# A mixer's projection products interleaved across units, and the k multiply of a level ahead of its copies

## The chip, the cores and the metric

The kernel runs on one core of a Trainium2 chip. The metric is the device time of one launch in microseconds, the median of several runs. TensorE (PE in the profile) does matmuls into eight PSUM banks of 128x512 f32, VectorE (DVE) and ScalarE (ACT) empty them, GpSimd (POOL) does further elementwise work, and SyncE (SP) issues most of the DMAs. Each engine runs its own list of instructions in order and waits on semaphores for the others.

## The reference

One layer on 2048 rows of width 1024: a norm and one input projection, two mixers on its columns, gates, an output projection, and a gated feed-forward network. Cut to what matters here:

```python
D_MODEL, SEQ, DEPTH = 1024, 2048, 1
def layer(x):
    z = rmsnorm(x, g) @ W_in            # [pool u | q | f | v | output gate | branch gates]
    a = pool_mixer(u, pool_w, pool_scale)      # trailing means over 2, 4, 8, 16 rows, less the row
    h = hgrn2_mixer(q, f, v, o, lb, norm_g)    # 4 heads: S_t = diag(f_t) S_{t-1} + (1-f_t) v_t^T
    m = sigmoid(ga) * (a @ W_pa) + sigmoid(gb) * (h @ W_pb)
    x = x + m @ W_out
    x = x + (silu(conv(n @ W_gate)) * conv(n @ W_val)) @ W_down    # n = rmsnorm(x, g2)
    return x
```

Inside the second mixer the decay between two rows is the product of the f between them, so attention within a chunk needs q and k scaled by running products of f.

## The kernel before, in words

The 2048 rows are worked in two passes of 1024, `b0` = 0 and 2, each of two halves of 512 rows. A pass runs a mixer and then the feed-forward part. Products of large matrices are made in units of the seven-product kind: a 2x2 block product from seven products P1 to P7 of sums of blocks, instead of eight. Each product is twelve matmuls of 128x512, since every operand is split in a high and a low fp32r part.

**The projections** of a mixer are 14 such units in the order of `PROJ` (L55): `fq` (f and q of a head), `g` (gates) and `u` (pool input). Before the change a unit runs through `ORDER` (L52): P1 P6 P5 P7 P2 P4 P3. P1 and P2 use one PSUM bank (X), P6, P7 and P4 a second (Z), P5 and P3 a third (V), and a bank gathers. `Unit.multiply` (L1172) issues a product and `Unit.after` (L1191) what follows it: behind P1, ACT copies e1 out of X (L1194); behind P6, VectorE makes u2 = e1 - Z (L1196); behind P7, u3 = Z - e1 (L1200) and one result, u3 + V (L1159). P7 adds into the bank that u2 reads, so it waits for u2; P4 waits for u3 in the same way.

**Weights** come as a stream (class `Stream`, L168): a load of 128x512 into one of 8 places (`raw`), in the first pass for some products a sum of blocks on POOL (L444), and then a split: ACT's cast to the high part (L231) and VectorE's subtract for the low part (L232), into a ring of 6 places (`ops`). A place comes free when the product that used it has ended. `plan_mixer` lists in which order the stream delivers. The second pass reads back the sums that the first one stored.

**Tasks** run between the products. After every sixth matmul of `mm` (L148) a tick steps the stream and each task. `hgrn_task` (L965) has a task for a head and a half: levels 1, 2, 4-8, 16-32 and 64 combine ever larger blocks of rows. At each level TensorE multiplies k and the scaled q into a bank (`pl`), VectorE copies pieces of it under masks into the attention matrix (`at`), and multiplies q, k and the decays (f) for the next level. `two_levels` (L993) does levels 4 and 16, in two pairs of banks, `pl.._0` and `pl.._2`. Behind the levels come `pk` (k transposed), `pv`, the states `ss`, the outputs `po`, their scaling `ot` (L1138) and a transpose `pt` (L1144). The pool's tasks make window sums `s` (L934), `p` (L939), its split `pl_g` (L657), and the product `pm`, and store `mx`.

**The end of the projections.** From the last unit on, `pa_task` loads the pool results again (`mx`, L961) and splits them (`mxs`, L656, L657), and the branch products `pa` and `pb`, chains of twelve matmuls, follow.

Names of tiles end in the half and the head or the group: `ur0_0` is unit u of group 0 in the first pass, `pl1_0_16_2` level 16 of head 0 in half 1, its second pair. In the profile the numbers are left out.

**The order on each engine** is made by a scheduler: it walks the program, simulates a timeline and puts each engine's instructions in the order in which they would become ready. Dependencies ahead of a task's product (`in_turn`, `first`, `behind`) pin some of it.

## Time and profile before

| what | us |
|---|---|
| median of 3 runs (2533.47 to 2534.64) | 2533.51 |
| the profiled execution, its own time | 2532.39 |
| its span in the profile | 2530.7 |
| projections of the first mixer, 98.15 to 454.70 | 356.55 |
| projections of the second mixer, 1358.90 to 1705.50 | 346.60 |

The granted clock of TensorE is 0.999 over the span. In the rows of the profile a line gives the engine, the line of the kernel, the operation, what is written and read (without numbers), shape and count; in a timeline the start and the time of the group stand first, and the square bracket holds the idle time before it and the engine that ended it. Matmuls overlap by their pipelining, so the steps from start to start count, not a record's own duration. The two windows hold the projections and what runs beside them; the second ends with the first `pa` chains.

### The profile page before, as it was taken

Reading aid. Unit: us, or ns where it says so; the run is one execution under the profiler, and the core shown is the slowest. Engines: PE = TensorE matmul, PEld = TensorE weight load, DVE = VectorE, ACT = ScalarE, POOL = GpSimd, SP = SyncE. Lnnn points to the kernel's source line nnn. Section 1 sums busy time; section 2 is a strip of 40 time slices with the busy share of each in tenths; the row PEclk is TensorE's granted clock in tenths of the full one; section 3 lists DMA queues with packets and bytes.
Section 4 is the critical chain, followed back from the end, with each engine's and each line's share of the span. In section 5 each row is a group of like instructions: output and inputs, shape, how many; then the busy total and the mean of one; then the engine's idle time right before and its main releaser. Section 6 shows DMA issues by size and latency. Waiting matters only on the chain.

```text
span 2530.7 us, 35649 instructions
## 1 busy us (share of the span) xinstructions
PE 2509.1 (99%) x11508; PEld 2053.6 (81%) x11508; DVE 1978.5 (78%) x3508; ACT 1176.1 (46%) x2218; POOL 753.4 (30%) x1127
## 2 busy tenths in 40 slices
PE   9999999999999999999999999999999999999998
PEld 7888888788888888888888888888888888888886
DVE  7889878598898777885596778765979888778755
ACT  6534343334555454554554343442355554445534
POOL 4344453003354334451320202200033432325410
PEclk9999999999999999999999999999999999999999
DMA  8878777777898879897344343446443454447852
GB/s 270 272 180 233 202 206 231 219 230 244 199 260 228 229 230 241 261 366 243 124 147 150 112 132 108 139 146 225 149 155 117 151 154 135 152 134 245 321 166 97
DMA packets 252332, 493.76 MB, mean 195 GB/s; under 512 B 26544, under 2 KB 43056, under 8 KB 251824
## 3 DMA queue, kind: packets, MB, share of 16 engines
q1 hardware_dynamic: 184512, 313.60, 39.1%
q0 software_dynamic: 42656, 112.74, 17.6%
q10 hardware_dynamic: 24976, 65.13, 7.6%
q8 instruction: 91, 1.49, 0.2%
q14 instruction: 97, 0.79, 0.1%
HBM read 381.79 MB, written 187.17 MB: 225 GB/s over the span
## 4 chain that ended last, share of the span: by engine, by line
PE 91%; DVE 5%; issue 1%; DMA 1%; POOL 1%; ACT 1%; SPq 0%; DVEq 0%; POOLq 0%; ACTq 0%
PE dn_P L148 16%; PE up_Z L148 14%; PE up_X L148 10%; PE up_V L148 10%; PE wo_P L148 6%; PE gr_Z L148 4%; PE pb L148 4%; PE pa L148 3%; PE io_Z L148 3%; PE gr_X L148 3%; PE fr_Z L148 2%; PE gr_V L148 2%; PE io_V L148 2%; PE fr_X L148 2%; PE fr_V L148 2%; PE pl L1026 1%
## 5 line engine op out<-in xcount | busy, mean ns | idle before, releaser
L231 ACT CAST ops<-raw 128x512 fp32r<-128x512 f32 x744 | 459.7, 620 | 817.8 <-PE dn_P L148 177.4
L232 DVE TENSOR_TENSOR ops<-raw,ops 128x512 fp32r<-128x512 f32 x744 | 553.0, 747 | 216.3 <-ACT ops L231 208.4
L1614 DVE SCALAR_TENSOR_TENSOR e<-h,cols,e 128x512 f32<-128x512 f32 x176 | 143.2, 818 | 30.9 <-ACT e L1612 26.3
L1612 ACT ACTIVATE e<-h,cols 128x512 f32<-128x512 f32 x176 | 142.3, 814 | 25.1 <-DVE h L1159 18.2
L1617 DVE SCALAR_TENSOR_TENSOR e<-h,cols,e 128x512 f32<-128x512 f32 x176 | 133.9, 770 | 2.5
L961 POOL DMA_DIRECT2D g_P<-dg_P x154 | 83.8, 545 | 160.3 <-PE dn_P L148 114.1
L1269 POOL TENSOR_TENSOR gf_P<-e,e 128x512 f32<-128x512 f32 x44 | 61.2, 1392 | 150.4 <-DVE e L1623 96.2
L1269 POOL TENSOR_TENSOR gf_P<-gf_P,e 128x512 f32<-128x512 f32 x44 | 59.1, 1344 | 72.0 <-DVE e L1623 71.5
L1409 POOL TENSOR_TENSOR q<-q,qs 128x512 f32<-128x512 f32 x16 | 21.7, 1357 | 185.2 <-ACT qs L1408 178.7
L1607 POOL COPY h<-h 128x2 f32<-128x2 f32 x88 | 40.8, 476 | 117.3 <-DVE h L1158 110.4
L1446 ACT ACTIVATE gt<-gt,cols 128x512 f32<-128x512 f32 x48 | 34.8, 725 | 86.8 <-DVE gt L1159 71.5
L1621 ACT ACTIVATE e<-e 128x512 f32<-128x512 f32 x88 | 55.6, 632 | 38.9 <-DVE e L1617 38.7
L1609 POOL COPY hist<-h 128x2 f32<-128x2 f32 x88 | 35.0, 398 | 117.6 <-DVE h L1159 115.8
L1159 DVE TENSOR_TENSOR h<-up_u,up_V 128x512 f32<-128x512 f32 x88 | 60.0, 682 | 10.2 <-PE up_V L148 9.7
L1244 DVE TENSOR_TENSOR x<-x,wo_P 128x512 f32<-128x512 f32 x88 | 56.0, 680 | 12.1 <-PE wo_P L148 11.9
L1244 DVE TENSOR_TENSOR ac<-ac,dn_P 128x512 f32<-128x512 f32 x72 | 47.1, 681 | 16.7 <-PE dn_P L148 16.5
L1011 POOL COPY qm<-q 128x64 f32<-128x64 f32 x64 | 29.9, 494 | 96.2 <-issue 25.9
L1026 PE MATMUL pl<-qm,k 128*128 128x192 f32 x256 | 50.6, 327 | 3.7 <-DVE k L1047 3.5
L1637 POOL DMA_DIRECT2D dg_P<-gf_P x88 | 50.7, 576 | 8.3 <-POOL gf_P L1269 7.4
L1607 POOL COPY h<-hist 128x2 f32<-128x2 f32 x88 | 45.0, 518 | 27.4 <-DVE m_T42l L657 27.3
L1194 ACT COPY up_e<-up_X 128x512 f32<-128x512 f32 x44 | 25.8, 586 | 58.2 <-PE up_X L148 53.1
L1026 PEld LDWEIGHTS pl<-qm,k 128*128 128x128 f32 x256 | 43.9, 189 | 9.6 <-POOL u L925 2.2
(1285 smaller groups left out, 8088.0 us busy)
## 6 DMA issues: line engine op xcount, KB each, us to landing
g_P<-dg_P POOLq DMA_DIRECT2D x154, 256.0 KB, 6.2
raw<-in_w_up_t SPq DMA_DIRECT2D x132, 256.0 KB, 3.2
raw<-in_w_in_t SPq DMA_DIRECT2D x98, 256.0 KB, 3.5
dg_P<-gf_P POOLq DMA_DIRECT2D x88, 256.0 KB, 4.0
dg_P<-e SPq DMA_DIRECT2D x66, 256.0 KB, 3.6
raw<-in_w_dn SPq DMA_DIRECT2D x66, 256.0 KB, 3.9
x<-in_x SPq DMA_DIRECT2D x64, 256.0 KB, 4.9
gd<-gt ACTq DMA_DIRECT2D x64, 256.0 KB, 3.2
```

The lines of the kernel that those rows point to most:

```text
L148: count[1] = pe.matmul(*args, **kw)
L231: self.mark = act.copy(hi, v)
L232: low = self.low = dve.tensor_tensor(lo, v, f32(hi), ALU.subtract)
L961: eng.dma_start(t, d)
L1026: ins = pe.matmul(pa_[:, c * 192 : c * 192 + 192], ks[:, (i + c) * P : (i + c + 1) * P], mv[:, c].rearrange("p s x -> p (s x)"), start=Tru ...
L1159: return dve.tensor_tensor(dst, t, ps, ALU.add if how == "add" else ALU.subtract)
L1244: dve.tensor_tensor(t, t, ps[j], ALU.add if sg > 0 else ALU.subtract)
L1269: pin(eng.tensor_tensor(t, x0, x1, op))
L1607: pool.tensor_copy(h[:, 0:2], hist[:, mt] if hf == 0 else hs[s, 0][:, TB : TB + 2])
L1612: in_turn(act.activation(t, h[:, 2:], AF.Identity, bias=col(o_cb + mt), scale=col(o_cw + 4 * MF + mt)))
L1614: in_turn(second(dve.scalar_tensor_tensor(t, h[:, 1 : 1 + TB], col(o_cw + 2 * MF + mt), t, ALU.mult, ALU.add)))
L1617: dve.scalar_tensor_tensor(t, h[:, 0:TB], col(o_cw + mt), t, ALU.mult, ALU.add)
```

## The change

Three edits in one file. The list `UNITS` gives the order of all the products of a mixer: P1 of the first unit, and then for each unit P6 P5 P2 P7, P1 of the next unit, P4 P3. The last unit keeps P6 P5 P7 P2 P4 P3. Two products stand between P6 and P7 in place of one, and between P7 and P4 the next unit's P1. The weight plan walks the same list. `pa_task` starts behind P6 of the last unit and no longer behind its P1, since P1 now lies in the unit before.

In `two_levels` the q multiply and the small products of decays move ahead of the `pl` products, to the operands; the k multiply is cut in two halves, each right behind its pair of `pl`, and the masked copies come after both. At levels 1, 2 and 64 the k multiply comes first, q and the decays follow, then the copies, with the two copies in the other order.

```diff
+UNITS = [(0, "P1")]
+for _n in range(len(PROJ) - 1):
+    UNITS += [(_n, "P6"), (_n, "P5"), (_n, "P2"), (_n, "P7"), (_n + 1, "P1"), (_n, "P4"), (_n, "P3")]
+UNITS += [(len(PROJ) - 1, p) for p in ORDER[1:]]
...
-        for kind, i in PROJ:
-            if (kind, i) == ("u", 0):
-                plan_one("pw", pool_wt)
-            plan_unit("in", w_in_t, kind, i, ORDER, b0)
+        units = {}
+        for n, p in UNITS:
+            kind, i = PROJ[n]
+            if n not in units:
+                if (kind, i) == ("u", 0):
+                    plan_one("pw", pool_wt)
+                mv, mg = proj_tiles(kind, i)
...
+            fn, raws = units[n][p]()
+            stream.op("in", fn, raws)
...
+            dve.tensor_tensor(qq[:, :, 1, :], qq[:, :, 1, :],
+                              dd[:, :, 0, 0:1].to_broadcast(full), ALU.mult)
+            dve.tensor_tensor(dd[:, :, 2, 0:1], dd[:, :, 2, 0:1], dd[:, :, 3, 0:1], ALU.mult)
+            dve.tensor_tensor(dd[:, :, 1, 0:1], dd[:, :, 1, 0:1], dd[:, :, 2, 0:1], ALU.mult)
+            dve.tensor_tensor(dd[:, :, 0, 0:1], dd[:, :, 0, 0:1], dd[:, :, 1, 0:1], ALU.mult)
             yield AHEAD
...
                 yield 1
+                half = slice(i * nb, (i + 2) * nb)
+                dve.tensor_tensor(kk[:, half, 0:3, :], kk[:, half, 0:3, :],
+                                  dd[:, half, 1:4, 0:1].to_broadcast([P, 2 * nb, 3, hh]),
+                                  ALU.mult)
+            for i, ps in zip(range(0, NT, 2), pls):
+                cc = slice(i, i + 2)
                 dve.copy_predicated(av[:, cc, :, 1, :], mask(hh, 2),
                                     ps[:, :, 0].rearrange("p c (b h) -> p c b h", h=hh))
...
-            if lv < 2:
-                dve.copy_predicated(av[:, :, :, 1, :], mask(hh, NT), pv4)
...
+            dve.tensor_tensor(k3[:, :, 0, :], k3[:, :, 0, :],
+                              d3[:, :, 1, 0:1].to_broadcast(full), ALU.mult)
             if lv:
                 dve.tensor_tensor(q3[:, :, 1, :], q3[:, :, 1, :],
                                   d3[:, :, 0, 0:1].to_broadcast(full), ALU.mult)
-            dve.tensor_tensor(k3[:, :, 0, :], k3[:, :, 0, :],
-                              d3[:, :, 1, 0:1].to_broadcast(full), ALU.mult)
             dve.tensor_tensor(d3[:, :, 0, 0:1], d3[:, :, 0, 0:1], d3[:, :, 1, 0:1], ALU.mult)
+            if lv < 2:
+                pv4 = pa_.rearrange("p (c s x) -> p c s x", c=NT, s=2)
+                dve.copy_predicated(av[:, :, :, 1, :], mask(hh, NT),
+                                    pv4[:, :, 0].rearrange("p c (b h) -> p c b h", h=hh))
+                dve.copy_predicated(ad, masks[-1 - lv].to_broadcast([P, NT, 64]), pv4[:, :, 1])
...
-        for n, (kind, i) in enumerate(PROJ):
...
-            for p in ORDER:
-                u.multiply(p, forms, late)
-                u.after(p)
-                if n == len(PROJ) - 1 and p == "P1":
-                    quiet[0] = True
-                    mtask = Task(pa_task())
+        units = {}
+        for n, p in UNITS:
...
+            units[n].multiply(p, forms, late)
+            units[n].after(p)
+            if (n, p) == (len(PROJ) - 1, "P6"):
+                quiet[0] = True
+                mtask = Task(pa_task())
```

Lines of the changed kernel stand some five to ten further down: u2 L1205, u3 L1209, the split L236 and L237, k L1049, the copies L1054 and L1057, `ot` L1147, `pt` L1153, the window sum L939 and p L944.

Three places of the engines' orders. First VectorE at level 16 of head 0 in the first mixer; `at0_0` and `at1_0` are the attention matrices of the two halves, `k0_0` and `k1_0` their k. Before:

```order
247 L1037 COPY_PREDICATED at0_0_1456<-m129_1144,pl0_0_16_0_1808 128x4x32
248 L1034 COPY_PREDICATED at1_0_1470<-m16_976,pl1_0_16_0_1811 128x8x16
249 L232 TENSOR_TENSOR ops50_1839<-raw49_1428,ops50_1839 128x512
250 L1037 COPY_PREDICATED at0_0_1456<-m128_1119,pl0_0_16_0_1808 128x4x32
251 L1037 COPY_PREDICATED at1_0_1470<-m129_1144,pl1_0_16_0_1811 128x4x32
252 L1034 COPY_PREDICATED at0_0_1456<-m16_976,pl0_0_16_2_1823 128x8x16
253 L1047 TENSOR_TENSOR k0_0_1453<-k0_0_1453,f0_0_1390 128x8x48
254 L1034 COPY_PREDICATED at1_0_1470<-m16_976,pl1_0_16_2_1829 128x8x16
255 L1037 COPY_PREDICATED at1_0_1470<-m128_1119,pl1_0_16_0_1811 128x4x32
256 L1047 TENSOR_TENSOR k1_0_1467<-k1_0_1467,f1_0_1436 128x8x48
```

After:

```order
249 L1049 TENSOR_TENSOR k0_0_1471<-k0_0_1471,f0_0_1361 128x4x48
250 L1054 COPY_PREDICATED at0_0_1474<-m16_976,pl0_0_16_0_1833 128x8x16
251 L1057 COPY_PREDICATED at0_0_1474<-m129_1144,pl0_0_16_0_1833 128x4x32
252 L1049 TENSOR_TENSOR k1_0_1485<-k1_0_1485,f1_0_1455 128x4x48
253 L1054 COPY_PREDICATED at1_0_1488<-m16_976,pl1_0_16_0_1836 128x8x16
254 L1057 COPY_PREDICATED at0_0_1474<-m128_1119,pl0_0_16_0_1833 128x4x32
255 L1057 COPY_PREDICATED at1_0_1488<-m129_1144,pl1_0_16_0_1836 128x4x32
256 L1057 COPY_PREDICATED at1_0_1488<-m128_1119,pl1_0_16_0_1836 128x4x32
257 L1049 TENSOR_TENSOR k0_0_1471<-k0_0_1471,f0_0_1361 128x4x48
258 L1054 COPY_PREDICATED at0_0_1474<-m16_976,pl0_0_16_2_1847 128x8x16
```

The whole k (128x8x48) of a half stood behind the copies of the first pair and behind one copy of the second; a half of k (128x4x48) now stands first behind each pair, and each pair's three copies behind it.

Second VectorE at unit f1 of the first mixer; `p1_0`, its low part `pl1_0l` and the next sum `s1_1_2` are the pool's, `fr0_1_u3` is what P4 of the unit waits for. Before:

```order
286 L939 SCALAR_TENSOR_TENSOR p1_0_2076<-s1_0_1_1975,u1_0_1959 128x512
287 L1117 SCALAR_TENSOR_TENSOR st0_1_123<-ss0_0_2061,f0_0_1390,pv0_0_2056 128x128
288 L232 TENSOR_TENSOR ops56_2041<-w56s4_2038,ops56_2041 128x512
289 L232 TENSOR_TENSOR ops57_2073<-raw53_1704,ops57_2073 128x512
290 L657 TENSOR_TENSOR pl1_0l_2079<-p1_0_2076,pl1_0h_2078 128x512
291 L934 TENSOR_TENSOR s1_1_2_2082<-s1_1_1_1979 128x512
292 L1200 TENSOR_TENSOR fr0_1_u3_2091<-fr0_1_Z_2003,fr0_1_e1_2001 128x512
293 L1159 TENSOR_TENSOR q1_1_2093<-fr0_1_u3_2091,fr0_1_V_2031 128x512
```

After:

```order
294 L237 TENSOR_TENSOR ops58_2109<-w58s2_2106,ops58_2109 128x512
295 L237 TENSOR_TENSOR ops59_2142<-w58s1_2103,ops59_2142 128x512
296 L237 TENSOR_TENSOR ops60_2189<-raw56_1831,ops60_2189 128x512
297 L944 SCALAR_TENSOR_TENSOR p1_0_2112<-s1_0_1_2005,u1_0_1990 128x512
298 L662 TENSOR_TENSOR pl1_0l_2115<-p1_0_2112,pl1_0h_2114 128x512
299 L939 TENSOR_TENSOR s1_1_2_2118<-s1_1_1_2009 128x512
300 L1209 TENSOR_TENSOR fr0_1_u3_2126<-fr0_1_Z_1992,fr0_1_e1_1928 128x512
301 L1168 TENSOR_TENSOR q1_1_2128<-fr0_1_u3_2126,fr0_1_V_2033 128x512
```

`p1_0` stood ahead of a state (`st0_1`) and two splits; now it stands behind three splits, and its low part, the next sum and u3 follow it directly.

Third VectorE at the end of the first mixer's projections; `ot0_3` and `ot1_3` are the outputs of head 3 in the two halves, `ops` the low parts of splits, `mxs` those of the pool results. Before:

```order
787 L232 TENSOR_TENSOR ops132_4937<-raw98_4603,ops132_4937 128x512
788 L657 TENSOR_TENSOR mxs1_1l_4845<-mx1_1_4842,mxs1_1h_4844 128x512
789 L1138 SCALAR_TENSOR_TENSOR ot0_3_4854<-po0_3_4769,ro0_3_4784,z0_3_4703 128x128 x4
790 L1159 TENSOR_TENSOR gt1_0_7_4877<-gr0_7_u2_4674,gr0_7_V_4676 128x512
791 L657 TENSOR_TENSOR mxs1_2l_4885<-mx1_2_4882,mxs1_2h_4884 128x512
792 L657 TENSOR_TENSOR mxs1_3l_4891<-mx1_3_4888,mxs1_3h_4890 128x512
793 L1519 TENSOR_TENSOR ya0_0_4924<-gl0_0_0_4894,pa0_0_4906 128x512
794 L232 TENSOR_TENSOR ops133_5014<-raw99_4660,ops133_5014 128x512
795 L232 TENSOR_TENSOR ops134_5053<-raw100_4689,ops134_5053 128x512
796 L1138 SCALAR_TENSOR_TENSOR ot1_3_4957<-po1_3_4859,ro1_3_4874,z1_3_4787 128x128 x4
```

After:

```order
807 L662 TENSOR_TENSOR mxs1_2l_4878<-mx1_2_4875,mxs1_2h_4877 128x512
808 L662 TENSOR_TENSOR mxs1_3l_4884<-mx1_3_4881,mxs1_3h_4883 128x512
809 L237 TENSOR_TENSOR ops133_5021<-raw99_4662,ops133_5021 128x512
810 L1147 SCALAR_TENSOR_TENSOR ot0_3_4917<-po0_3_4806,ro0_3_4821,z0_3_4737 128x128 x4
811 L1530 TENSOR_TENSOR ya0_0_4940<-gl0_0_0_4887,pa0_0_4899 128x512
812 L1530 TENSOR_TENSOR ya0_4_4964<-gl0_0_4_4891,pa0_4_4946 128x512
813 L237 TENSOR_TENSOR ops134_5069<-raw100_4699,ops134_5069 128x512
814 L1147 SCALAR_TENSOR_TENSOR ot1_3_4988<-po1_3_4922,ro1_3_4937,z1_3_4824 128x128 x4
```

`ot0_3` stood behind `ops132`, and both `ops133` and `ops134` between it and `ot1_3`; now it stands behind `ops133`, and `ops134` alone is ahead of `ot1_3`.

More of the change, by code (lines that the diff above doesn't have):

```diff
@@ L390, in plan_io @@
                 stream.op("io", fn, raws)
-    def plan_unit(key, src, kind, i, order, b0):
-        mv, mg = proj_tiles(kind, i)
-        if b0:
-            unit = sums_of_unit(src, mv, mg, lambda p: lambda: kept["in", (kind, i), SUM_OF[p]])
-        else:
-            unit = weights_of_unit(src[mv], src[mg], (kind, i))
-        for p in order:
-            fn, raws = unit[p]()
-            stream.op(key, fn, raws)
     def plan_mixer(b0):
         plan_io(b0)
-        for kind, i in PROJ:
-            if (kind, i) == ("u", 0):
-                plan_one("pw", pool_wt)
-            plan_unit("in", w_in_t, kind, i, ORDER, b0)
+        units = {}
[5 more added lines that the diff above has]
+                mv, mg = proj_tiles(kind, i)
+                if b0:
+                    units[n] = sums_of_unit(w_in_t, mv, mg, lambda p, u=(kind, i): (
+                        lambda: kept["in", u, SUM_OF[p]]))
+                else:
+                    units[n] = weights_of_unit(w_in_t[mv], w_in_t[mg], (kind, i))
+            fn, raws = units[n][p]()
+            stream.op("in", fn, raws)
         for key, src in (("pa", w_pa_t), ("pb", w_pb_t)):
@@ L1473, in mixer @@
         mixed, oT = {}, {}
[L1474 to L1483 removed]
+        units = {}
+        for n, p in UNITS:
+            kind, i = PROJ[n]
+            if n not in units:
+                if (kind, i) == ("u", 0):
+                    held["w"] = stream.get("pw")
+                units[n] = Unit(f"{kind[0]}r{b0}_{i}", "in", emits[kind](i))
+            units[n].multiply(p, forms, late)
[3 more added lines that the diff above has]
+                mtask = Task(pa_task())
         def branch(key, s, xs, evac, each):
```

25 lines of the change are left out of this document (6 added, 19 removed).

## The prediction

> **What bounds the kernel now.** I read the page first: busy times and the chain of waits.
>
> ```profile
> PE 2509.1 (99%) x11508; PEld 2053.6 (81%) x11508; DVE 1978.5 (78%) x3508; ACT 1176.1 (46%) x2218; POOL 753.4 (30%) x1127
> ...
> PE 91%; DVE 5%; issue 1%; DMA 1%; POOL 1%; ACT 1%; SPq 0%; DVEq 0%; POOLq 0%; ACTq 0%
> ```
>
> TensorE is busy 2509.1 of 2530.7 us and carries 91% of the chain, VectorE 5%. The change adds and removes no product, so it can win only time in which TensorE stands still: 21.6 us in the whole execution. Next came a table of stages, for the two stretches that the change reorders, the projections of the first mixer and of the second.
>
> ```profile
> core 0: us, PE busy (x) PEld busy (x) DVE busy (x) ACT busy (x) POOL busy (x), PEclk, DMA share, GB/s
> 98.15:454.70 356.55, 351.11 (x1777) 292.08 (x1776) 299.33 (x679) 142.59 (x320) 143.13 (x151) 1.00 0.78 218
> 1358.90:1705.50 346.60, 346.52 (x1770) 291.13 (x1769) 258.01 (x665) 143.64 (x317) 59.17 (x86) 1.00 0.43 129
> ```
>
> The columns are the stretch, its length and the busy time of each engine. The first mixer leaves TensorE 5.4 us idle (356.55 less 351.11), the second 0.1. The prize therefore lies in the first mixer, where VectorE is busy 84% of the time and POOL makes the weight sums that the second mixer only reads back. The waits of TensorE in that stretch (total, times, longest) name its releasers.
>
> ```profile
> PE pl L1026 <- DVE k L1047: 3.5, 2, 1.8
> PE ur_Z L148 <- DVE ur_u L1196: 1.1, 1, 1.1
> PE gr_Z L148 <- DVE gr_u L1200: 0.4, 1, 0.4
> PE fr_Z L148 <- DVE fr_u L1196: 0.3, 1, 0.3
> ```
>
> The second mixer has no such row. Two kinds of wait carry the loss: the level products `pl` for the k multiply, and P7 for u2.
>
> **The k multiply.** One of the two places in order of time:
>
> ```profile
> 150.08 1.31 POOL L444 TENSOR_TENSOR w51s<-raw,raw 128x512 f32<-128x512 f32 x1 [1.53 <-issue]
> 150.13 1.29 DVE L1046 TENSOR_TENSOR f<-f 128x8 f32<-128x8 f32 x1
> 151.76 1.26 DVE L1045 TENSOR_TENSOR f<-f 128x8 f32<-128x8 f32 x1
> ...
> 152.94 0.28 DVE L1037 COPY_PREDICATED at<-m,pl 128x128 f32<-128x128 uint8 x1
> 153.13 0.28 DVE L1034 COPY_PREDICATED at<-m,pl 128x128 f32<-128x128 uint8 x1
> 153.33 0.55 DVE L1047 TENSOR_TENSOR k<-k,f 128x384 f32<-128x384 f32 x1
> ...
> 154.02 0.89 PE L1026 MATMUL pl<-qm,k 128*128 128x192 f32 x4 [1.77 <-DVE k L1047]
> 154.40 0.16 DVE L1049 TENSOR_TENSOR f<-f 128x8 f32<-128x8 f32 x1
> ```
>
> VectorE runs without a gap here: two multiplies of 8 columns take 1.29 and 1.26 us beside POOL's sum, where a like one alone takes 0.16. Two masked copies (0.28 each) then stand ahead of k, which ends at 153.88, and TensorE has waited 1.77. The other place shows the same figure (3.5 for two). The change puts k ahead of the copies, gives it the first half of the operands only, and takes the q multiply and the small decays off the piece between. I price the removal at 3.8: at least the 3.5 of the view, at most 4.3, since the view counts from a modelled matmul end.
>
> The split adds instructions. A half has 192 columns; the nearest rows are the whole k (384 columns, mean 682 ns) and the q multiply of 128 columns (295).
>
> ```profile
> L1047 DVE TENSOR_TENSOR k<-k,f 128x384 f32<-128x384 f32 x16 | 10.9, 682 | 0.0
> ...
> L939 DVE SCALAR_TENSOR_TENSOR p<-s,u 128x512 f32<-128x512 f32 x8 | 6.2, 773 | 2.5 <-DMA kwfq1ins<-w53s 2.1 <-PE pm L949 0.4
> ...
> L1043 DVE TENSOR_TENSOR q<-q,f 128x128 f32<-128x128 f32 x16 | 4.7, 295 | 0.0
> ...
> L657 DVE TENSOR_TENSOR pl_1l<-p,pl_1h 128x512 fp32r<-128x512 f32 x2 | 1.4, 692 | 0.1
> ```
>
> Between them a half is about 0.39, two halves 0.1 more than the whole: 16 multiplies add 1.6 us of VectorE to a stage in which it has 57 us free. That is hidden, except where VectorE has no slack. Such places remain: the copies, now last, are what gives the level's PSUM bank back. In head 0 the changed order puts 39 VectorE instructions between the first `pl` of level 4 and the bank's release for the last of level 16. At the undisturbed durations of the rows (0.16 for a small decay, 0.28 a copy, 0.39 a half of k, 0.68 a split or u2) they come to about 12.4 us, an estimate, against 12.7 us of matmul steps on TensorE, so one hit of 1.1 us by a POOL sum (1.29 less 0.16 above) shows. Heads 0 and 3 run their two sequences side by side in this way. I charge 0.8 for each, 1.5 in all; bounds 0 (no hit) to 3.5 (the old wait by another name).
>
> **u2 and P7.** The largest of these waits:
>
> ```profile
> 308.67 0.39 PE L148 MATMUL ur_V<-x_T13h,ops 128*128 128x512 f32 x1
> 308.90 0.39 PE L148 MATMUL ur_V<-x_T13l,ops 128*128 128x512 f32 x1
> ...
> 310.02 0.62 DVE L1037 COPY_PREDICATED at<-m,pl 128x128 f32<-128x128 uint8 x2
> 310.55 0.68 DVE L1196 TENSOR_TENSOR ur_u<-ur_e,ur_Z 128x512 f32<-128x512 f32 x1
> ...
> 311.29 0.50 PE L148 MATMUL ur_Z<-x_T30h,ops 128*128 128x512 f32 x1 [1.11 <-DVE ur_u L1196]
> ```
>
> Products step by 0.23 us a matmul (308.67 to 308.90), so twelve take 2.8. u2 starts at 310.55, behind copies, and P7 at 311.29 instead of about 310.2. With P5 and P2 both between P6 and P7, u2 has 2.8 us more. The largest lateness is 1.1, so the wait goes everywhere: 1.4 by the view (1.1 and 0.3), and up to 2.4, as 1.0 more of TensorE's 5.4 idle us has no other name; I take 1.8. P4's distance to u3 stays one product, since P1 of the next unit takes the place that P2 had: the 0.4 of `gr_u` L1200 stays.
>
> **What comes in its place.** The new order also moves the tasks that run between the products. Four places lose cover.
>
> First, the last unit's transposes. Before, one column group of `pt` waits behind two weight splits whose ring place comes free only at the end of a `pa` chain:
>
> ```profile
> 464.23 1.14 ACT L231 CAST ops<-raw 128x512 fp32r<-128x512 f32 x2 [3.25 <-PE pa L148]
> 464.88 1.29 DVE L232 TENSOR_TENSOR ops<-raw,ops 128x512 fp32r<-128x512 f32 x2 [2.58 <-ACT ops L231]
> ...
> 466.09 1.12 DVE L1138 SCALAR_TENSOR_TENSOR ot<-po,ro,z 128x128 f32<-128x128 f32 x4
> 466.49 0.33 PE L1144 MATMUL pt<-ident,ot 128*128 128x128 f32 x1 [1.84 <-DVE ot L1138]
> ```
>
> From the cast (464.23) to `pt` (466.49) are 2.26 us, of which TensorE idles 1.84. After the change this place has a long cover, but `ot0_3` stands behind one such split and `pt0_3` directly behind the `pa1_0` that frees it: one cast, one subtract, one `ot`, thus 2.26 less the second subtract's 0.6, or 1.65, and the distance is nil. I take 1.7, bounds 1.2 to 1.9. In the first mixer this replaces 1.84 (net -0.1); in the second mixer `ot2_3` and `pt2_3` stand in the same way and nothing is given back: +1.7.
>
> Second, P4 of unit g4. Its u3 stands behind a window sum. Before:
>
> ```profile
> 342.85 0.70 DVE L934 TENSOR_TENSOR s<-s 128x524 f32<-128x524 f32 x1
> ...
> 343.59 0.69 DVE L1200 TENSOR_TENSOR gr_u<-gr_Z,gr_e 128x512 f32<-128x512 f32 x1
> ...
> 343.99 0.39 PE L1127 MATMUL po<-st,q 128*128 128x128 f32 x2
> ...
> 344.21 0.39 PE L1125 MATMUL po<-v,at 128*128 128x128 f32 x2
> ...
> 344.35 0.48 PE L148 MATMUL gr_Z<-x_T40h,ops 128*128 128x512 f32 x1
> ```
>
> From the sum's start to P4 are 1.50 us, and TensorE was just not late. In the changed order this sum waits for the last of `po0_2`, with two steps of 0.22 us (343.99 to 344.21) and the product's own between: 0.67 of cover. I charge 1.0; bounds 0 (if the sum's input has been free longer) to 1.5.
>
> Third, P4 of unit f1: p, its cast, its low part, the next sum and u3 now follow `po0_0` in one queue: 0.77, about 0.62 (a cast, 464.23 above, two in 1.14), 0.69, 0.70 and 0.69 from the rows, with some 0.2 of hand-over 3.7 us, against 2.5 us of `pv`, `po` and `pm` steps. +1.2; bounds 0 to 1.5.
>
> Fourth, the `mx` loads start one product later, because their task now starts at P6 of the last unit.
>
> ```profile
> 454.29 0.68 DVE L232 TENSOR_TENSOR ops<-raw,ops 128x512 fp32r<-128x512 f32 x1
> ...
> 455.42 0.88 SPq L961 DMA_DIRECT2D mx<-md  x2
> ...
> 459.69 0.62 ACT L656 CAST mxs_2h<-mx 128x512 fp32r<-128x512 f32 x1 [0.94 <-DMA mx<-md]
> ...
> 460.34 0.69 DVE L657 TENSOR_TENSOR mxs_2l<-mx,mxs_2h 128x512 fp32r<-128x512 f32 x1 [2.36 <-ACT mxs_2h L656]
> ```
>
> ```profile
> DMA to landing us min/median/max: 2.9/4.2/5.1
> ```
>
> Before, the third load is issued behind a split's subtract (454.29) at 455.42 and its low part is ready at 461.03, 5.6 us on. That split is paced by the last product of the unit in both orders: a cast of 0.62 and three VectorE steps of 0.6 lie between, so I estimate 2.5 from the unit's end to the issue, and 8.1 to the part. `pa1_0` comes after two whole `pa` chains and eight `po` steps (2.8 + 2.8 + 1.8) and needs the part in its seventh or eighth matmul, at 9.0, when it has been ready for 0.9 us; the next part follows 0.7 us after it, with half a microsecond to spare. With the longest landing (5.1 against 4.3 from 455.42 to 459.69) that one is late by 0.3. I charge 0.3 for both mixers; bounds 0 to 4.
>
> The SP queue is otherwise moved only with the products that pace it, and so are POOL's sums, which follow the stream in the new order of use.
>
> **The sum.** -3.8 -1.8 -0.1 +1.7 +1.0 +1.2 +1.5 +0.3 = 0.0. The profiled execution took 2532.39 us (span 2530.7), 1.1 under the median of the runs, 2533.51; the difference is put on that median: **2533.5 us**. With each term at its bound nearest to gain the sum is -6.1 (-4.3 -2.4 -0.6 +1.2), nearest to loss +7.6 (-3.5 -1.4 +0.1 +1.9 +1.5 +1.5 +3.5 +4).
>
> **The rivals.**
>
> The new waits don't come. What speaks for it: each of the four rests on durations in one queue, and a term falls where that queue has run ahead. Against: the two splits at the `pa` end are freed by the very chain that `pt` follows. With the two `ot` waits alone: -3.8 -1.8 -0.1 +1.7, or 2529.5; with the second mixer's away too, 2527.8.
>
> VectorE becomes the bound in the level stretches of the first mixer: slower. Place: heads 0 and 3, levels 4 to 16 and 16 to 64, four stretches. A POOL sum that meets both halves of k there costs 2.2, and as the copies follow, the bank comes back later by as much; four stretches give 8.8 in place of my 1.5, or 2540.8. It decides from three of the four. For it: 84% busy. Against: the mean k of 0.682 is only 0.13 over the 0.55 of an undisturbed one, and POOL works 143 of 357 us. The Trainium skill, Perfetto Trace Analysis, section Optimizing Scalar/DVE Operations, has a rule that speaks for it: GpSimd and VectorE share a read port of SBUF. By that rule alone each added half of k is exposed once more to a POOL sum, and the time would come out as this rival gives it. The 1.29 beside a sum against 0.16 alone agrees with the rule; the mean of k does not show it often.
>
> The `mx` loads are late by a whole product more, as the queue that issues them waits for one more split: 2.8 less the half microsecond to spare is 2.3 in each mixer, 4.6 in place of my 0.3, or 2537.8. Against it: the same split paces them.
>
> The change doesn't do what it says: u2 stays late, because on VectorE it is queued behind the same copies. Then 1.8 comes back: 2535.3. Against: two products are 5.6 us.
>
> **How the numbers follow.** Forecast 0.56 (own range 2530.5 to 2536.5), the new waits don't come 0.17, VectorE the bound 0.13, late loads 0.09, no effect on u2 0.05. A difference under 0.2%, 5.1 us (2528.4 to 2538.6), can't be told from none. Of the second case 0.11 lies below that; of the third 0.13 above, and 0.02 of the fourth. So faster 0.11, same 0.74, slower 0.15. The range is 2528.0 to 2539.0: below, the gains with nearly all of the new waits gone, above, VectorE the bound in three stretches.
>
> **What would show it.** In the waits of TensorE in the first mixer the rows for k and for u2 are gone or under 0.5 together, one for u3 of 1 to 3 us is there, and `pt` waits for `ot` once in each mixer, about 1.7. A row of `pl` waiting for the copies (now L1054 and L1057) under 2 us is the residue; over 5 us it is the second rival. TensorE's idle time in the first mixer's stretch stays within 1 us of 5.4. The prediction is wrong if the `ot` rows are missing, or if the second mixer's stretch gains a wait that none of these terms names.

## The result, and the profile after

The changed kernel takes 2549.80 us (median of 6 runs, 2547.35 to 2555.57), the kernel before 2533.49 beside it (2532.82 to 2535.22). The ratio is 1.0064 with a 95% interval of 1.0054 to 1.0074: slower by 16 us, where 2533.5 was forecast. The profiled execution took 2548.52 us, 16.1 more than the profiled one of before, and so do the spans (2546.8 against 2530.7).

The busy times of the changed kernel:

```profile
PE 2515.5 (99%) x11508; PEld 2060.4 (81%) x11508; DVE 1979.9 (78%) x3540; ACT 1179.6 (46%) x2218; POOL 746.9 (29%) x1127
```

The same 11508 matmuls make TensorE busy 6.4 us longer (2515.5 against 2509.1); the other 9.7 us are idle time. Both come from one stage. The projections of the first mixer, in a table of stages (the stretch, its length, the busy time of each engine, the granted clock of TensorE):

```profile
core 0: us, PE busy (x) PEld busy (x) DVE busy (x) ACT busy (x) POOL busy (x), PEclk, DMA share, GB/s
98.15:470.00 371.85, 356.08 (x1761) 295.24 (x1760) 299.80 (x698) 145.03 (x320) 138.75 (x150) 0.98 0.74 209
```

TensorE idles 371.85 less 356.08, or 15.8 us, against 5.4 before: 10.3 more. And the clock column, 1.00 before, is 0.98. Where it falls shows in short windows of the same view:

```profile
166.80:171.80 5.00, 4.80 (x14) 3.82 (x15) 3.76 (x11) 0.25 (x2) 0.00 (x0) 0.66 0.83 207
196.00:201.00 5.00, 4.90 (x19) 4.22 (x20) 4.78 (x9) 2.18 (x11) 1.49 (x1) 0.70 0.18 52
245.40:250.40 5.00, 4.90 (x15) 3.79 (x16) 5.00 (x23) 0.08 (x1) 0.00 (x0) 0.66 1.07 195
401.00:406.00 5.00, 5.00 (x24) 4.67 (x25) 5.00 (x14) 2.25 (x5) 0.00 (x0) 0.72 1.04 204
329.40:334.40 5.00, 4.98 (x27) 4.03 (x28) 4.90 (x16) 1.27 (x3) 0.31 (x1) 1.00 0.00 0
360.30:365.30 5.00, 5.00 (x22) 4.09 (x23) 4.51 (x11) 3.79 (x13) 3.90 (x5) 1.00 0.66 157
```

Each window begins where TensorE has just waited. Behind four of these six waits its clock is 0.66 to 0.72 over five microseconds. The missing parts (0.34, 0.30, 0.34 and 0.28 of 5 us) make 6.3 us. TensorE is counted busy meanwhile, since each matmul takes longer. The wait at 167.0, ahead of the first window, is of 1.5 us alone, with one of 0.5 some two microseconds before it; the other three are of 2.0 to 2.9. The two waits without a slow stretch behind them are of 1.9 and 1.0. So 10.3 of waiting and 6.3 of slow matmuls, 16.6 together, are the loss up to the end of the first mixer; there the first `pb` product starts at 516.8 in place of 500.4, 16.4 later. The second mixer adds 1.3 (its first product starts 15.6 later, its first `pb` 16.9), and about 0.8 comes back by the end, which I did not follow.

What TensorE waits for in that stage (total, times, longest), the answer to the four rows of before:

```profile
PE pl L1040 <- DVE at L1057: 3.8, 3, 2.0
PE pl L1075 <- DVE q L990: 2.9, 1, 2.9
PE pm L952 <- ACT pl_0h L661: 2.6, 1, 2.6
PE gr_X L153 <- DVE at L1057: 1.9, 1, 1.9
PE gr_Z L153 <- DVE gr_u L1209: 1.7, 2, 1.0
PE pt L1153 <- DVE ot L1147: 1.7, 1, 1.7
PE ur_Z L153 <- DVE ur_u L1209: 1.5, 1, 1.5
PE pl L1040 <- ACT ops L236: 0.8, 2, 0.5
PE pl L1085 <- DVE k L1049: 0.5, 1, 0.5
```

The waits that the change aimed at are nearly gone: k was 3.5 and is 0.5, and the rows of u2 (1.1 and 0.3) have no successor. Without `pt`, which lies behind the stage, the new rows sum to 15.7, which is its idle time. Nearly all name VectorE. Two of the largest, in order of time. First the wait for q at the start of head 3 (from a timeline, VectorE and POOL):

```profile
394.81 1.55 DVE L978 TENSOR_SCALAR f<-f,lbt 128x512 f32<-128x512 f32 x1 [0.36 <-ACT f L1413]
...
396.03 1.48 POOL L449 TENSOR_TENSOR w113s<-w107s,raw 128x512 f32<-128x512 f32 x1
396.28 1.78 DVE L237 TENSOR_TENSOR ops<-w110s,ops 128x512 fp32r<-128x512 f32 x1
...
397.98 2.50 DVE L237 TENSOR_TENSOR ops<-raw,ops 128x512 fp32r<-128x512 f32 x1
398.10 1.81 POOL L449 TENSOR_TENSOR w114s<-raw,raw 128x512 f32<-128x512 f32 x1
...
400.40 0.41 DVE L990 TENSOR_TENSOR q<-q,f 128x256 f32<-128x256 f32 x1
```

VectorE has no gap between 394.81 and 400.40, but two splits that take 0.68 alone take 1.78 and 2.50 beside POOL's sums. That is 2.9 us more than alone, and TensorE then waits 2.9 for q, which stands behind them. At 245.4, where `pl` waits 2.0 for the copies, a multiply of 128 columns takes 2.31 us in place of 0.32 beside the sums of w72s.

Second the wait of `pm` at 196.1:

```profile
189.58 1.28 POOL L449 TENSOR_TENSOR w58s<-raw,raw 128x512 f32<-128x512 f32 x1 [5.48 <-DMA kwfq1ins<-w57s]
...
192.90 1.29 DVE L237 TENSOR_TENSOR ops<-w58s,ops 128x512 fp32r<-128x512 f32 x2 [2.99 <-ACT ops L236]
...
194.71 0.69 DVE L944 SCALAR_TENSOR_TENSOR p<-s,u 128x512 f32<-128x512 f32 x1
195.43 0.62 ACT L661 CAST pl_0h<-p 128x512 fp32r<-128x512 f32 x1 [1.52 <-DVE p L944]
```

Here VectorE is idle (2.99 us), and late for another reason: `p` stands behind the splits of w58s in its queue, and the sum w58s waited 5.48 us until the store of w57s gave it a slot.

### The profile page after: what moved, and what is told of

It is laid out like the page before. It is cut to its first block, busy times and chain, and to the rows that moved or that the text cites. A ratio compares the mean times of both kernels' runs of the same rounds, so it can differ in the third digit from the quotient of the medians.

```text
span 2546.8 us, 35682 instructions
## 1 busy us (share of the span) xinstructions
PE 2515.5 (99%) x11508; PEld 2060.4 (81%) x11508; DVE 1979.9 (78%) x3540; ACT 1179.6 (46%) x2218; POOL 746.9 (29%) x1127
## 4 chain that ended last, share of the span: by engine, by line
PE 90%; DVE 5%; DMA 2%; issue 1%; ACT 1%; POOL 1%; SPq 0%; ACTq 0%; POOLq 0%; DVEq 0%
PE dn_P L153 16%; PE up_Z L153 14%; PE up_V L153 10%; PE up_X L153 10%; PE wo_P L153 6%; PE gr_Z L153 4%; PE pb L153 3%; PE pa L153 3%; PE io_Z L153 3%; PE gr_V L153 3%; PE gr_X L153 2%; PE fr_Z L153 2%; PE io_V L153 2%; PE fr_V L153 1%; PE fr_X L153 1%
## 5 line engine op out<-in xcount | busy, mean ns | idle before, releaser
L236 ACT CAST ops<-raw 128x512 fp32r<-128x512 f32 x744 | 459.9, 621 | 800.7 <-PE dn_P L153 178.3
L237 DVE TENSOR_TENSOR ops<-raw,ops 128x512 fp32r<-128x512 f32 x744 | 555.7, 750 | 228.4 <-ACT ops L236 223.3
L1253 DVE TENSOR_TENSOR ac<-ac,dn_P 128x512 f32<-128x512 f32 x72 | 47.2, 683 | 16.7 <-PE dn_P L153 16.4
```

What stands on the lines that cost most here:

```text
L236: self.mark = act.copy(hi, v)
L237: low = self.low = dve.tensor_tensor(lo, v, f32(hi), ALU.subtract)
L1253: dve.tensor_tensor(t, t, ps[j], ALU.add if sg > 0 else ALU.subtract)
```

## The experiments

Sixteen kernels, in the order of the questions. Where parts are left out, the text says so once. Times are medians, differences against the runs of the kernel before beside them.

**Which edit costs the time?** The two parts of the change apart. e1 has the product order and none of the edits in the levels; e2 has the edits in the levels and the old order of products.

```diff
 e1: the changed kernel, levels as before
-            dve.tensor_tensor(qq[:, :, 1, :], qq[:, :, 1, :],
-                              dd[:, :, 0, 0:1].to_broadcast(full), ALU.mult)
...
-                dve.tensor_tensor(kk[:, half, 0:3, :], kk[:, half, 0:3, :],
...
+            dve.tensor_tensor(kk[:, :, 0:3, :], kk[:, :, 0:3, :],
+                              dd[:, :, 1:4, 0:1].to_broadcast([P, nb, 3, hh]), ALU.mult)
 e2: the changed kernel, order as before
-        for n, p in UNITS:
...
+        for n, (kind, i) in enumerate(PROJ):
...
+            for p in ORDER:
```

> The order of the products alone, the levels as before. Theory A (the level edits make VectorE late with the copies that give banks back, and this is most of the loss): the u2 waits go (-1.4), the pool's product waits for its low part and the ot waits come, about 2535 to 2539. Theory B (the product order is the cause: weight sums and splits come late because slots are held longer): 2543 to 2550, with the waits of pm for pl_0h (2.6) and of the first level for q (2.9) as in the change and slow matmul steps of 0.43 us behind them.

> The level edits alone, the products in the old order. Theory A: slower than before, 2540 to 2546, with waits of pl or of a product for at L1057 of 4 to 8 us and a clock below 1.00 in the stretch. Theory B: faster, 2529 to 2532, since the waits for k (3.5) go and nothing comes in their place.

e1 took 2550.27 (ratio 1.0066, 1.0049 to 1.0082), e2 2539.01 (1.0018, 1.0008 to 1.0027), both against 2534.04. The product order alone loses the whole 16 us, as the second of the two theories said; the levels alone lose 5, less than the first theory said and not the gain of the second. Together they are no worse than the order alone: the parts don't add. In e1 the waits of TensorE in the first mixer are partly those of before, made longer:

```profile
PE pl L1031 <- DVE k L1052: 6.4, 4, 2.6
PE pl L1071 <- DVE q L990: 2.9, 1, 2.9
PE pm L952 <- ACT pl_0h L661: 2.8, 1, 2.8
```

So the level edits do what they were made for (6.4 for k falls to 0.5), and the copies take the place of k. In e2 the waits for k are gone too, and others stand there instead:

```profile
PE ur_Z L148 <- DVE ur_u L1200: 2.5, 2, 1.6
PE pl L1070 <- DVE q L985: 2.2, 1, 2.2
PE pt L1148 <- DVE ot L1142: 1.8, 1, 1.8
PE gr_Z L148 <- DVE gr_u L1200: 1.6, 1, 1.6
```

e12 asks for the smallest edit of this kind: the old order of products, and only the group of q, decays and whole k moved ahead of the second pair's copies.

```diff
                 yield 1
+                if i == NT - 2:
...
+                    dve.tensor_tensor(kk[:, :, 0:3, :], kk[:, :, 0:3, :],
+                                      dd[:, :, 1:4, 0:1].to_broadcast([P, nq, 3, hh]), ALU.mult)
...
                 dve.copy_predicated(av[:, cc, :, 1, :], mask(hh, 2),
```

> The old order; in the two-level steps only the group of q, decays and the whole k moves ahead of the second pair's three copies; no split, no other level touched. If k ahead of the copies is good by itself: 2529 to 2532, the k waits (3.5) gone, little new. If whatever stands ahead of the copies makes them late by as much: 2534 to 2538, with waits for u2 or for at in place of those for k.

It took 2534.34 against 2533.68, ratio 1.0001 (0.9991 to 1.0010). The k wait shrinks from 3.5 to 0.9, and waits for u2 (2.2 and 1.4), qm (1.0) and the copies (0.8) come instead. That is the second of the two outcomes expected: moving k ahead moves the wait on.

**Does the place of P1 and P7 matter, or any new order?** e3 has the levels as before and runs P6 P5 P7 P2, the next P1, P4 P3.

```diff
-    UNITS += [(_n, "P6"), (_n, "P5"), (_n, "P2"), (_n, "P7"), (_n + 1, "P1"), (_n, "P4"), (_n, "P3")]
+    UNITS += [(_n, "P6"), (_n, "P5"), (_n, "P7"), (_n, "P2"), (_n + 1, "P1"), (_n, "P4"), (_n, "P3")]
```

> Levels as before; P6 P5 P7 P2, the next unit's P1, P4 P3: one product again between P6 and P7, two between P7 and P4. e1 lives as long as in the change, u2 as before. If the longer life of e1 (slots) is what makes the sums late, this is as slow as the order of the change alone. If the place of P7 or the chance of the scheduler's order is, it differs from it by over 3 us. The u3 waits (0.4 before) go, the u2 waits (1.4) stay.

It took 2566.19 against 2534.04, 1.0124 (1.0109 to 1.0139): 32 us slower, though it gives P4 two products of distance. Its waits in the first mixer are `ot` 7.7 (with `pt` behind the stage), u2 7.6, a decay f 5.4 and qm 3.6, all on VectorE. The order differs from that of the run e1 only in the places of P2 and P7, the copy e1 of a unit lives as long in it, and it is 16 us slower still. So neither the distance between a product and its result nor the life of that copy decides alone. The waits point to VectorE; why they are larger here than in e1 was not followed.

**Is it the work on VectorE, and what POOL does beside it?** e5 and e6 make no weight sums at all, in the old and in the new order: blocks go to the splits in their place, no slot is used or stored for them, and the second pass loads blocks. e7 and e8 keep slots and stores, but a copy on ScalarE stands for each sum of POOL.

```diff
 e5, e6
-            rs = [raw(i) for i in {"P1": (0,), "P2": (1,), "P4": (3,), "P6": (0, 2, 3),
-                                   "P7": (0, 2), "P3": (1,)}[p]]
+            rs = [raw(i) for i in {"P1": (0,), "P2": (1,), "P4": (3,), "P6": (0, 2, 3),
+                                   "P5": (2,), "P7": (0, 2), "P3": (1,)}[p]]
...
-                if p == "P6":
-                    comb(nm, "s1", t[1], t[2])
-                    return comb(nm, "s2", tmp["s1"], t[0])
...
                 return t[0]
 e7, e8
             t = slot(f"{nm}{key}")
-            pool.tensor_tensor(t, x0, x1, ALU.add)
+            act.copy(t, x0)
```

> The old order of products without the weight sums: P5, P6, P7 and P3 take one of the blocks in place of the sum, no sum is made on POOL, stored or read back (the second pass loads the blocks). It is the base for the next run. All theories: at or a little under 2534, the waits for k and u2 mostly gone, since VectorE meets no sum on POOL.

> The same without the weight sums in the new order of products (levels as before). The order alone cost +16 with the sums. If the sums are the way by which it costs (late because slots are held longer, or in VectorE's way), it stands within 4 us of the base without sums, the 1.7 of the new pt wait in each pass among it. If the order costs by itself (PSUM banks held longer, products in worse places between the levels), it is 8 us or more over that base.

> The old order with the sums' slots, stores and timing kept, but ScalarE copies one block in place of POOL's add, so that POOL doesn't hold VectorE (the sum is not made). The base for the next run: at or under 2534.

> The new order of products with copies on ScalarE in place of the sums (slots and stores as in the change; the sum is not made). If slots are the cause, it is 8 us or more over the base with the same copies, with waits for stores on the engine that now makes them. If POOL's sums slowing VectorE are the cause, it is within 4 us of the base.

| weight sums | old order | new order (levels as before) | difference |
|---|---|---|---|
| on POOL, stored (before, e1) | 2534.04 | 2550.27 | +16.2 |
| on POOL, not stored (e10, e11) | 2530.09 | 2547.28 | +17.2 |
| ScalarE copies in their place, stored (e7, e8) | 2524.40 | 2532.15 | +7.8 |
| none (e5, e6) | 2520.75 | 2526.51 | +5.8 |

Without sums the new order costs a third of what it costs with them, with ScalarE's copies half. Both differences lie between the bounds that were set for them (within 4 us the sums are the way, from 8 us on they are not), so these four kernels alone say that the sums are the larger part and not the whole. The runs of e6 spread from 2523.0 to 2526.9, and its profiled execution is only 2.9 us over that of e5. In e6 TensorE has one row left in the first mixer,

```profile
PE pt L1140 <- DVE ot L1134: 1.7, 1, 1.7
```

and the same 1.7 in the second, where e5 has none: the two waits for `ot` that were forecast, 3.4 together, cover the 2.9 of the profiled executions and 3.4 of the 5.8 of the medians. In e8 a wait of `pm` for `pl_0h` (2.4) comes on top.

What the sums do shows in the stretches from the first to the last `pl` of each head in the first mixer. In the kernel before (VectorE's is the third of the busy times, behind PE and PEld):

```profile
123.00:163.00 40.00, 38.23 (x202) 32.22 (x201) 39.12 (x111) 12.91 (x28) 15.26 (x19) 1.00 0.80 209
202.30:246.60 44.30, 43.93 (x228) 36.43 (x226) 43.61 (x118) 16.36 (x35) 17.33 (x19) 1.00 0.86 232
279.20:324.10 44.90, 43.79 (x228) 36.44 (x227) 44.09 (x116) 15.33 (x33) 16.95 (x21) 1.00 0.65 190
380.90:421.80 40.90, 38.98 (x202) 32.07 (x202) 40.73 (x106) 11.26 (x26) 16.91 (x18) 1.00 0.90 255
sum 170.10, PE 164.92 PEld 137.16 DVE 167.55 ACT 55.86 POOL 66.46; mean PE 41.23 PEld 34.29 DVE 41.89 ACT 13.96 POOL 16.61
```

VectorE is busy 167.55 of 170.10 us there, more than TensorE. The slack over the whole stage (57 us) lies elsewhere. The sums of the four like stretches in the changed kernel:

```profile
sum 168.10, PE 160.92 PEld 133.87 DVE 161.75 ACT 57.30 POOL 66.17; mean PE 40.23 PEld 33.47 DVE 40.44 ACT 14.32 POOL 16.54
```

in e5:

```profile
sum 164.20, PE 164.14 PEld 138.64 DVE 143.85 ACT 59.80 POOL 25.88; mean PE 41.04 PEld 34.66 DVE 35.96 ACT 14.95 POOL 6.47
```

and in e6:

```profile
sum 161.30, PE 161.30 PEld 136.68 DVE 141.03 ACT 59.73 POOL 27.80; mean PE 40.33 PEld 34.17 DVE 35.26 ACT 14.93 POOL 6.95
```

With the sums gone VectorE needs 144 us for the same work, and TensorE idles nowhere, in either order. Summed over the instructions that exceed the shortest of their kind, VectorE is held 46.9 us in 48 instructions in the first mixer of before, 43.6 in the changed kernel, and 5 to 6 in e5 to e8. In the four stretches alone the holds are 26.8 us before and 26.7 in the changed kernel, so the new order does not make more of them, and VectorE's reserve there is not smaller (161.75 of 168.10 us busy). What the new order changes is which instruction stands behind a hold. In the stretches TensorE idles 7.2 us in place of 5.2, and two large waits lie at their edges: that for q (2.9) just ahead of head 3's, that for u3 of the pool unit (1.5) just behind head 0's. That the holds fall at worse places is read from these places; the four sums do not show it.

**Or is it the stores and slots of the sums?** They could delay the weights. e10 and e11 keep POOL's sums and leave out only their stores (the second pass loads blocks and not their sums); e4 gives the changed kernel one slot more and pays for it with one of the 8 places of the weight stream; e9 takes one slot from the kernel before.

```diff
 e10, e11
             tmp[key] = t
-            keep(("in", unit, key), t)
 e4: the changed kernel
-N_SLOTS = 77
+N_SLOTS = 78
...
-N_RAW = 8
+N_RAW = 7
 e9: the kernel before
-N_SLOTS = 77
+N_SLOTS = 76
```

> The old order; the weight sums are made on POOL as before but not stored, and the second pass loads blocks in their place (its products are not the reference's). The base for the next run; about 2530 to 2534.

> The new order of products with the sums on POOL but not stored: their slots come free after use, without waiting for a store. If the stores and slots are what makes POOL's sums late and so dear, the difference to the base falls from 16 to 4 to 8 us. If it is that POOL's adds meet VectorE at worse moments in this order, it stays at 12 or more.

> The whole change with one slot more (78) and one place less in the ring of raw loads (7). Theory B: POOL's waits for stores that free slots (10.8, 8.7, 6.1, 5.5 us) shrink and the time falls by 3 us or more. Theory A: within 3 us of the change (2549.8), since copies and POOL sums on VectorE decide.

> The kernel before with 76 slots in place of 77. The new order holds e1 four products longer of the seven of a unit, u2 one: 0.7 slots on the average. If slots that come free late are the way by which the order costs, one slot less costs the old order too, 5 us or more, and POOL's waits for stores rise from 16 us towards 50. If not: within 3 us of 2534.

Without the stores the new order still costs 17.2 us, so the stores are not the way by which it loses: it stays over the 12 that were set for this. Nor do POOL's waits for stores go with the time: they are 42.8 us in the first mixer of e10, 15.8 in that of the kernel before, which is 3.6 us slower. e4 took 2555.47 (+21, and 5.7 over the change), which neither theory expected: POOL's waits for stores fall from 51.8 to 28.0 us in the first mixer, and others come, perhaps from the lost place of the stream. e9 took 2545.58 against 2533.68, 1.0051 (1.0035 to 1.0068): one slot of 77 less costs the old order 12 us, over the 5 that were set as the sign that late slots cost time, while POOL's waits for stores rise only from 15.8 to 24.8. So the kernel before stands at an edge in this too, and a slot can cost nearly as much as the order; what e11 shows is that the order's loss does not need the stores.

**What does a wait cost TensorE?** The four slow windows stand behind waits, and what a wait of a given length costs in all had not been measured. e13 to e16 set waits of chosen lengths where TensorE waits for nothing: in the second mixer of the kernel before, ScalarE copies the bank behind P7 of seven gate units 5, 6, 7 or 8 times into a place that nobody reads, and P4 waits for the last copy.

```diff
                 self.forms.setdefault("u3", []).append(ins)
+                if self.name[:3] == "gr2" and self.name != "gr2_7":
+                    hold = slot(f"{self.name}_hold")
+                    for _ in range(8):
+                        act.copy(hold, bk["Z"])
```

> In the second mixer, where TensorE waits for nothing in the kernel before, ScalarE copies the bank Z five times behind P7 of the seven gate units g0 to g6, and P4 has to wait for the last copy. Five copies of about 0.55 us are 2.8 us, about the length of P2 between: waits of 0 to 0.8 us each. Theory A (a wait over about 2 us makes TensorE run at half rate for some 3 us behind it, a shorter one does not): the loss is the sum of the waits, 0 to 5 us, no matmul step of 0.427 us. Theory B (a wait costs its own length at any size): the same.

> Six copies in place of five: waits about 0.6 us longer than in e13. Theory A and theory B: the sum of the waits, some 4 us above e13; no step of 0.427 us.

> Seven copies: waits about 1.2 us longer than in e13, 1.2 to 2. Theory A: still the sum of the waits, but for those that reach 2 us. Theory B: the sum of the waits.

> Eight copies: waits about 1.8 us longer than in e13, 1.8 to 2.6. Theory A: behind most of the seven waits some ten matmul steps of 0.427 us in place of 0.232, so about 2 us more for each than its length, 10 to 14 us above the sum of the waits. Theory B: seven times 0.6 us above e15 and no slow steps.

The inserted waits are 7.2 us in e13 (four, the longest 2.2). In e16 (total, times, longest):

```profile
PE gr_Z L148 <- ACT gr_hold L1206: 26.1, 7, 4.4
```

The stage that holds them, in e16, with its clock in the column PEclk as above:

```profile
1358.90:1740.00 381.10, 354.86 (x1729) 294.93 (x1728) 256.41 (x659) 169.69 (x360) 56.10 (x84) 0.96 0.37 112
```

The medians are 2547.28, 2559.32, 2566.99 and 2574.90, against 2534.33. The waits were longer than expected, as other work stood between the copies. In e16 the span is 42.2 us longer: 26.1 of waiting and, at a clock of 0.96 over 381 us, some 15 of slow matmuls, 41 together. One such place in e16:

```profile
1400.26 0.80 PE L148 MATMUL gr_Z<-x_T40h,ops 128*128 128x512 f32 x1 [3.67 <-ACT gr_hold L1206]
1400.86 0.63 PE L148 MATMUL gr_Z<-x_T40l,ops 128*128 128x512 f32 x1
1401.28 0.63 PE L148 MATMUL gr_Z<-x_T40h,ops 128*128 128x512 f32 x1
...
1405.12 0.63 PE L148 MATMUL gr_Z<-x_T43h,ops 128*128 128x512 f32 x1
1405.55 0.44 PE L148 MATMUL gr_V<-x_B220h,ops 128*128 128x512 f32 x1
1405.82 0.40 PE L148 MATMUL gr_V<-x_B220l,ops 128*128 128x512 f32 x1
1406.06 0.39 PE L148 MATMUL gr_V<-x_B220h,ops 128*128 128x512 f32 x1
```

From 1400.86 the starts are 0.427 us apart (from 1401.28 to 1405.12 nine steps), from 1405.82 again 0.24. Behind the three inserted waits of 1.2 to 1.8 us no step is slow, behind nine of the fourteen of 2.0 to 3.2 us six to eleven are, and behind all eight of 3.4 us or more six to thirteen, at 0.195 us each. So a wait can cost 1.2 to 2.5 us more than its length. That a wait always costs just its length, the rival of these four runs, is wrong; so is the sharp bound at 2 us of the theory.

What decides between waits of like length shows in where the clock falls. In e16 it falls at 1398.80, 1484.13, 1514.85, 1569.47, 1630.90, 1682.11 and 1712.83, steps of 25, 9, 16, 18, 15 and 9 times 3.413 us, and it stays at one half for 3.41 or 6.83 us. The falls of the other traces lie on such a grid too. Two waits, cut at the grid: one of 2.04 us in e14 that lies in one window, and one of 3.05 in e15 that lies across two.

```profile
1395.40:1398.81 3.41, 1.42 (x7) 0.81 (x5) 3.41 (x14) 3.19 (x10) 0.00 (x0) 1.00 0.41 156
1398.81:1402.22 3.41, 3.35 (x8) 2.68 (x9) 2.64 (x13) 0.53 (x2) 2.51 (x3) 0.50 0.09 32
```

```profile
1396.15:1399.56 3.41, 1.86 (x11) 1.24 (x9) 3.41 (x13) 3.20 (x10) 0.00 (x0) 1.00 0.39 147
1399.56:1402.97 3.41, 1.91 (x8) 1.61 (x9) 3.07 (x16) 1.45 (x3) 2.40 (x3) 1.00 0.20 77
```

In e14 TensorE idles 1.99 us of the first window, and the second is at half clock; in e15 it idles 1.55 and 1.50, and the clock stays. Over the 14 traces in which the clock falls, leaving out their first 20 and last 12 us, all 41 windows at full clock with 1.78 us or more idle are followed by half clock, and of the 10184 with 1.69 us or less one is (in e9); between the two, two of seven are, the one before the first slow stretch of the changed kernel (1.72) among them. So the idle time within a window counts, and half of the window is about the bound. A single wait of 1.70 in e1 set it off, and the wait of `pt` for `ot`, 1.84 in both traces, did so in e15 and not in the kernel before.

The Trainium skill, TensorE: Matmul & The Clock Gate, Part 1, says that a monitor halves TensorE's clock after an idle window of about 3.4 us, that this window runs freely, and that the clock comes back after a window as long of busy time. The starts that it states for 512 columns at half rate, 426.7 ns, are the 0.427 measured here, and its window is the 3.41 of the grid. Its 3.4 us as the gap to avoid is too long for this kernel: here half a window of idle time set it off.

## Why the prediction was wrong

**Right.** The waits for k and u2 went: a gain of 4.9 by the rows (3.5, 1.1 and 0.3), where 5.6 was charged, and 0.5 for k came back. The waits for `ot` came as priced: 1.7 in each mixer (the row of the whole changed kernel is 3.4, 2, 1.7). P4 of unit g4 waits 1.0, as charged.

```profile
PE pt L1153 <- DVE ot L1147: 3.4, 2, 1.7
```

The `mx` loads were on time, no row names them; the rivals of the late loads, of the new waits that don't come and of u2 that stays late fall. No wait came in the second mixer that the terms do not name. So neither of the two signs that the prediction set for its being wrong appeared, though it was.

**The step that failed: VectorE's slack.** The prediction said that the added work is hidden because VectorE has 57 us free over the stage, and charged 1.5 for the rest (heads 0 and 3 alone, bounds 0 to 3.5). The slack had to be counted in the level stretches, where it is 2.5 us of 170 and under 1 us in each of the four heads. In them and at their edges the new order lost 5.7 for the copies (3.8 of `pl` and 1.9 of the next unit's P1, which needs the bank), 2.9 for q, 1.5 for u3 of the pool unit, 0.7 for u3 of another unit and 0.5 for k: 11.3 in place of 1.5. The charge took one hit of 1.1 us by a sum for each of two heads; the holds in the four stretches are 26.7 us. e5 to e8 show that these waits need POOL's sums: without them TensorE waits in no stretch of e6, and in e8, which keeps the stores, 2.1 of such waits are left (1.1, 0.6 and 0.4). That the holds, and not sums that come late for want of a slot, are the way rests on e10 and e11 and on the places read above.

**The second rival named this mechanism, but half of its place and not its price.** It put the loss in heads 0 and 3; 3.9 of the 5.7 for the copies fall in heads 1 and 2. Its 2540.8 rested on the halves of k being hit, two for each stretch. They were not: 32 halves have a mean of 0.367 us, 0.34 alone. What was hit were splits (1.78 and 2.50) and level multiplies (2.31), and whatever stands behind them in the queue is late with them. With the adds taken off POOL, in e7 and e8, VectorE's holds fall from some 45 to 5 or 6 us, and the loss by the new order from 16.2 to 7.8. The rule of the Trainium skill, Perfetto Trace Analysis, section Optimizing Scalar/DVE Operations, that GpSimd and VectorE share a read port of SBUF, was cited for this rival; the holds agree with it, but no run here shows that the port is the way.

**A price that was missing: the clock.** 6.3 us of the loss are not waits. The four rows of before showed no wait over 1.9 us, and its clock is 1.00 in both mixers, so its trace could not show this price, and the sum charged each wait with its length alone. e13 to e16 measured it.

**P4 of unit f1** was charged 1.2 for the chain of p behind three splits. The place was right and the chain late, but `pm` met it first, and by 2.6 us with 1.5 of clock behind it: my 3.7 us begin with p, and leave out the splits that stand ahead of it, of which the first two wait for a sum, which waits 5.48 us for a slot. The queue order shows what stands ahead, not what that waits for.

**Two statements to withdraw.** The idle time of the stage was to stay within 1 us of 5.4, and it is 15.8. The copies' row, to be under 2 us or over 5, is 3.8 and 1.9: with the wait of the next unit's P1 for its bank it is 5.7, the side of the second rival.

**What stays open.** Why the holds fall worse in the new order is read place by place, not derived: the scheduler puts the sums elsewhere, and e2 (+5), e3 (+32) and e9 (+12) show that other edits of this stage lose too. How much of the loss the slots have is not parted from it: one slot less costs the old order 12 us by itself. About 2.4 of the 5.8 us of e6 over e5 stand in slower executions than the profiled one and have no row, and what the lost stream place costs in e4 was not tried apart. No kernel of this study that computes the whole beats the kernel before; e12 equals it.

## What to carry to other kernels

Look for an engine's slack in the stretch where it is needed, not over the stage: 16% free in the mean was 1.5% where the levels ran, and there each reorder that was tried turned one wait into another. Price the waits of the matmul engine with the clock: in this kernel, where over half of a window of 3.41 us was idle, up to 1.7 us came on top for each such window at half clock behind it, so a few long waits are worse than many short ones spread out. If one engine's work holds another, look at what its removal would give before a new order: the kernels that leave POOL's sums out are 9 to 13 us faster in the old order and 18 to 24 in the new.

## What the runs showed of the hardware that was not expected

TensorE runs at half rate (512 columns in 0.427 us in place of 0.232) for 3.41 or 6.83 us behind single waits as short as 1.7 us, in streams that hardly idle but for such waits (in e16 354.86 of 381.10 us busy, 26.1 in the waits). The falls lie on a grid of 3.41 us, and a wait sets one off where it leaves about half of one window idle; a wait of 3.05 that the grid cut into 1.55 and 1.50 did not. And a subtract of 128x512 on VectorE, 0.68 us alone, took 2.50 beside a POOL sum of 1.81: 0.68 and 1.81 are 2.49, as if the one had run after the other.
